# MLP of a two-layer decoder trunk: half of the up product's contraction as seven block products, and the residual summed in DRAM by accumulating transfers

## The chip, the cores and the metric

The kernel runs on one core of a Trainium2 chip. The metric is the time of one execution on the device, in microseconds; three executions are shown and their median is taken.

## The reference

A sequence of 1024 tokens, 1024 channels, everything in float32. Layer 0 mixes with a chunked mLSTM, layer 1 with differential attention over keys and values that are projected once after layer 0. Cut to what the change touches:

```python
def sq_relu_mlp(y, w_up, w_down):                 # w_up 1024x4096, w_down 4096x1024
    return jnp.square(jax.nn.relu(y @ w_up)) @ w_down

for layer in range(2):
    x = x + g1 * mix                              # mLSTM (layer 0), attention (layer 1)
    y = modulate(rms_norm(x, norm_mlp_g[layer]), sh2, sc2)
    x = x + g2 * sq_relu_mlp(y, mlp_w_up[layer], mlp_w_down[layer])
    if layer == 0:
        k1, k2, v = shared_kv(x, ...)             # k and v projections of the normed x
return rms_norm(x, final_norm_g)
```

## The kernel before

**Products.** A float32 value is kept as a rounded high part and the rest, both in the float32r type: `yh` and `yl` for activations, `wh` and `wl` for weights. A product of a 128x128 weight block and 512 tokens is three matmuls into one PSUM bank (`mm3`, lines 183 to 185): `wh` by high, `wh` by low, `wl` by high. The tokens are two halves of 512, the channels eight blocks of 128.

**MLP.** `mlp` goes through the 4096 hidden columns in eight groups of four 128-column tiles. Up phase of a group: four tiles by two halves by eight contraction blocks by three, 192 matmuls. The results go through relu and square (lines 613 and 614). In groups 1 to 7 the hidden values of a pair of tiles are a 2x2 matrix of blocks (tile by token half); `quad_out` forms the sums of blocks that a seven-product scheme for 2x2 matrices needs, and splits them into `bh`, `bl`, `th`, `tl`. `pair_load` does the same to a pair of weight tiles of `w_dn`: raw tiles `e` and `m`, four subtractions and additions of 256 columns (lines 654 to 657), and the splits `eh`, `el`, `lh`, `ll`. Down phase: four pairs `i` by seven products `p` by two contraction blocks by three, 168 matmuls in the order of `PSEQ`. Each product is added to the residual `xt`, which stays in SBUF, by one VectorE instruction on 512 columns (line 675), 28 in a group. Group 8 (the "last" one) uses plain `hh`, `hl`, and its down product goes through `gemm` once for each token half, loading and splitting its weights each time.

**Memory.** Weights pass through a ring of nine tiles of 128x1024 (`wp`); a tile of the ring also serves the modulation's background work (`adar`, line 150). Scratch tiles of 128x512 come from a ring of six (`np_`). PSUM has seven banks for products and one for norms. All loads and stores are issued on SP's queue; POOL has no work.

**Order.** The kernel is written in the order of its data; a scheduler then fixes one order of instructions for each engine, and an instruction waits on semaphores for its inputs and for its output's buffer. Nothing is reordered while it runs.

**Elsewhere.** After layer 0, `gemm` projects queries and then keys, tile order `QKORD`, first group of three tiles; `v_store` writes values to DRAM; `project_a` interleaves the output projection with attention.

Of the kernel before, what the change touches and what calls it, by code (L numbers as in the profile page):

```python
# [17 lines left out]
P = 128  # L18
# [8 lines left out]
FN = 4  # L27
# [3 lines left out]
        (1, 3), (2, 6), (1, 4), (2, 2), (3, 1), (2, 7), (3, 5), (2, 3), (3, 6), (2, 4), (3, 2), (3, 7), (3, 3), (3, 4))  # L31
AHEAD, LAG, FULL, FILL0 = 2, 2, 5, 3
CUT = 256
LSZ = (2, 2, 1, 3)
QKORD = (2, 3, 4, 0, 1, 5, 6, 7)
# [19 lines left out]
def tile_yoco(ctx: ExitStack, tc: tile.TileContext, x, c, pos, cst, vec, bg, lp, ada,  # L55
# [117 lines left out]
    def wload(src, shape, nbg=1, pool=None):  # L173
        r = wp.tile(shape, F32, tag="w", name="wraw")
        sp.dma_start(out=r, in_=src)
        h = (pool or wp).tile(shape, F32R, tag="w", name="wh")
# [29 lines left out]
    def gemm(srcs, nk, ah, al, consume, nbg=1, halves=(0, 1), first=2, hooks=None,  # L206
             after=None, joint=None, sizes=None):
# [5 lines left out]
        def load(g):  # L213
            return [wload(srcs[i], [P, nk, P], nbg) for i in g]
# [382 lines left out]
    def mlp(np_, l, xt, slot, nbg, ends, args, before=None, tail=None, closing=()):  # L597
# [3 lines left out]
        with ExitStack() as ph:  # L601
# [17 lines left out]

            quads = {}  # L620

            def quad_out(f, half, ps):
                j, q = f // 2, quads.setdefault(f // 2, {})
                q[f % 2, half] = squared(ps)
# [13 lines left out]
                if (1, 1) in q:  # L638
# [27 lines left out]

            moving = {1: (bh, bl, 0), 2: (bh, bl, 1), 3: (bh, bl, 2), 4: (th, tl, 3), 5: (th, tl, 0), 6: (th, tl, 1),
                      7: (th, tl, 2)}

            def down(pairs, ready):  # L670
                banks = {}

                def add(ps, half, nb):
                    xs = xt[:, int(half), nb]
                    dve.scalar_tensor_tensor(xs, ps, mcol(l, 5, nb), xs, ALU.mult, ALU.add)  # L675

                for i, p in PSEQ:
# [15 lines left out]
                    add(ps, p in (6, 7, 5, 3), 2 * i + (p in (7, 4, 5)))  # L693
# [27 lines left out]
            for gi in range(FG - 1):  # L721
                srcs = [[dn_src(gi, 2 * i + j, "(p q r c) -> p q r c", q=2, r=2) for j in range(2)] for i in range(4)]
                for got in group_up(gi, w0, steady if gi else first, lambda: pair_load(srcs[0])):
                    if isinstance(got, dict):
                        pairs = [got] + [lambda i=i: pair_load(srcs[i]) for i in range(1, 4)]
                    else:
                        quad_out(*got)
                nxt = []
                down(pairs, lambda: nxt.append(wload(w_up[l, FN * (gi + 1)], [P, NB, P], nbg and nbg + 1)))
                w0 = nxt[0]  # L730
# [3 lines left out]
            sums = hp.tile([P, 2, HT], F32, tag="bh", name="sums")  # L734
            acc[:] = [sums[:, 0], sums[:, 1]]
            srcs = [dn_src(FG - 1, nb, "(p k c) -> p k c", k=FN) for nb in range(NB)]
            gi = FG - 1
            for got in group_up(gi, w0, steady, lambda: None):
                if got is None:
                    continue  # L740
                f, half, ps = got
                r = scratch("r")
# [13 lines left out]
    def resident(ph, name):  # L756
# [5 lines left out]
        return xp.tile([P, 2, NB, HT], F32, tag="x", name="x"), np_  # L762
# [3 lines left out]
    xt, np_ = resident(l0, "1")  # L766
# [15 lines left out]
    def q_norm(half):  # L782
        def f():
            rb = rstd_of(np_, half)
            sp.dma_start(out=rdr[half:half + 1], in_=rb[0:1])
            modulate(np_, xt, rb, half, 3, lambda k: mcol(1, 0, k))
            sp.dma_start(out=xdr[:, half], in_=xt[:, half])
        return f

    mlp(np_, 0, xt, 1, 2, ((0,), (1,)), {(1,): dict(hooks={1: q_norm(0)})}, lambda: scale_cols(3, 48 + 8, V_NMIX + 8),  # L790
# [4 lines left out]

    rps = ExitStack()
    scr = rps.enter_context(tc.tile_pool(name="scr", bufs=2, side="right"))
    cos = scr.tile([P, T], F32, tag="cos", name="cos", bufs=1)
# [39 lines left out]
    def v_store(cc, scr):  # L838
        def f(tb, ps):
            v = scr.tile([P, 2, BV], F32, tag="sv", name="sv")  # L840
            act.copy(out=v, in_=ps.rearrange("p (h v) -> p h v", h=2))  # L841
            for j in range(2):
                sp.dma_start(out=vdr[2 * cc + j, :, tb], in_=v[:, j])
        return f

    q_out = rope_out(lambda s: qdr[:, s], float(BD ** -0.5))
# [6 lines left out]
    def kv_norm(half):  # L853
        return lambda: modulate(np_, xt, kvn[half], half, 2, lambda k: mod[:, 96 + k:97 + k])

    gemm([w_q[n] for n in QKORD], NB, yhk, ylk, q_out, first=3, joint=1,
         after={(3, 0): kv_norm(0), (3, 1): kv_norm(1)})
    gemm([w_kv[n] for n in QKORD], NB, yhk, ylk, rope_out(lambda s: kdr[s], 1.0), first=3, joint=1)
# [22 lines left out]
    with ExitStack() as ph:  # L881
# [6 lines left out]
        identr = ap_.tile([P, P], F32R, tag="identr", name="identr", bufs=1)  # L888
        negr = ap_.tile([P, P], F32R, tag="negr", name="negr", bufs=1)
        neg = ap_.tile([P, P], F32, tag="neg", name="neg", bufs=1)  # L890
        sp.dma_start(out=neg, in_=cst[:, C_NEG])
        act.copy(out=identr, in_=ident)
        act.copy(out=negr, in_=neg)
# [67 lines left out]
        def values(h, qb):  # L961
# [11 lines left out]
            sq = ap_.tile([P, BV], F32, tag="sq", name="sq")  # L973
# [245 lines left out]
```

## Time and profile before

| what | value |
|---|---|
| median of three runs | 2427.49 us (2426.15 to 2429.11) |
| the profiled execution | 2429.98 us, its span 2428.2 us |
| mean granted TensorE clock | 0.991 |
| TensorE busy | 2367.1 us, 12018 matmuls and transposes |
| VectorE busy | 1559.4 us, 2576 instructions |
| ScalarE busy | 989.2 us, 1898 instructions |
| POOL busy | 0.2 us, 4 instructions |
| DMA | 266.81 MB, 110 GB/s on average, all on SP's queue |

The page gives busy time and share of the span by engine, the chain of work that ended last, and groups of instructions with their count, busy time, mean duration in ns, the idle time ahead of them and what ended it. Mean durations include latency that overlaps the next instruction; the pace of an engine is seen from start to start. "PEclk" or the number behind the last engine's busy time is the granted share of TensorE's clock.

### The profile page before, as it was taken

The page shows a single profiled execution, that of the slowest core. Times are in us where ns is not written, and L with a number is a line of the kernel's source. Part 1 is how long each engine was busy: PE and PEld are TensorE (multiplying, and loading weights), DVE is VectorE, ACT ScalarE, POOL GpSimd, SP SyncE. Part 2 cuts the span into 40 slices and gives each one's busy share as a digit, 9 for nine tenths or more (in the row PEclk, how much of TensorE's full clock was granted, in tenths as well). Part 3 has the DMA queues.
Part 4 walks back from the last instruction along what each step waited for, and adds up shares of the span by engine and source line. Part 5 has one row for each costly group of instructions (what it writes and reads, how often), then busy time and mean ns, then how long its engine had stood idle before and what let it go on. Part 6 is the DMA issues. An engine that isn't in the chain of part 4 may idle for free.

```text
span 2428.2 us, 30918 instructions
## 1 busy us (share of the span) xinstructions
PE 2367.1 (97%) x12018; PEld 1983.7 (82%) x12018; DVE 1559.4 (64%) x2576; ACT 989.2 (41%) x1898; POOL 0.2 (0%) x4
## 2 busy tenths in 40 slices
PE   7999999999999999999999999999999999999997
PEld 4899998788888888887788899987778888878886
DVE  7436544787877787767653367664775567566647
ACT  4325633444324323424332467763434323432423
POOL 0000000000000000000000000000000000000000
PEclk9999999999999999999999999999999999999999
DMA  7312242313322342234454654764111111111113
GB/s 306 120 64 77 79 148 78 122 51 119 135 95 79 130 139 75 90 113 143 153 178 154 176 162 148 217 196 160 65 57 35 61 61 44 39 61 57 35 53 122
DMA packets 117150, 266.81 MB, mean 110 GB/s; under 512 B 12426, under 2 KB 51850, under 8 KB 115212
## 3 DMA queue, kind: packets, MB, share of 16 engines
q1 hardware_dynamic: 117004, 264.84, 33.5%
q8 instruction: 94, 1.54, 0.3%
q14 instruction: 52, 0.43, 0.1%
HBM read 228.03 MB, written 36.77 MB: 109 GB/s over the span
## 4 chain that ended last, share of the span: by engine, by line
PE 90%; DVE 3%; DMA 3%; ACT 2%; issue 1%; SPq 1%; DVEq 0%; ACTq 0%
PE gps L183 24%; PE gps L185 24%; PE gps L184 24%; PE gps L255 3%; PE gps L256 3%; PE gps L257 3%; PE gps L971 2%; PE sc L930 1%; PE sc L931 1%; PE tps L957 1%; DMA kb<-kdr 1%; DVE adar L336 1%; PE hps L528 1%; DMA wraw<-in_w_do_dram 1%; PE hps L530 1%
## 5 line engine op out<-in xcount | busy, mean ns | idle before, releaser
L183 PE MATMUL gps<-yh,wh 128*128 128x512 f32 x1664 | 657.4, 399 | 7.9 <-ACT yh L301 5.0
L184 PE MATMUL gps<-yl,wh 128*128 128x512 f32 x1664 | 658.5, 396 | 0.7 <-DVE yl L302 0.7
L185 PE MATMUL gps<-yh,wl 128*128 128x512 f32 x1664 | 655.3, 396 | 0.7 <-DVE wl L171 0.7
L183 PEld LDWEIGHTS gps<-yh,wh 128*128 128x128 f32 x1664 | 313.6, 189 | 85.4 <-ACT yh L301 5.9
L185 PEld LDWEIGHTS gps<-yh,wl 128*128 128x128 f32 x1664 | 313.4, 188 | 78.7 <-DVE wl L171 1.1
L184 PEld LDWEIGHTS gps<-yl,wh 128*128 128x128 f32 x1664 | 313.5, 188 | 76.7 <-issue 1.2
L170 ACT CAST wh<-wraw 128x1024 fp32r<-128x1024 f32 (+2 forms) x176 | 170.6, 970 | 473.7 <-DMA wraw<-in_w_up_dram 208.9
L171 DVE TENSOR_TENSOR wl<-wraw,wh 128x1024 fp32r<-128x1024 f32 (+2 forms) x176 | 198.1, 1126 | 206.3 <-ACT wh L170 204.5
L675 DVE SCALAR_TENSOR_TENSOR x<-gps,mod,x 128x512 f32<-128x512 f32 x392 | 286.8, 746 | 59.7 <-PE gps L185 58.1
L255 PE MATMUL gps<-wh,yh 128*128 128x256 f32 (+1 forms) x768 | 224.9, 293 | 4.8 <-ACT sv L841 3.4
L256 PE MATMUL gps<-wl,yh 128*128 128x256 f32 (+1 forms) x768 | 220.6, 287 | 0.0
L257 PE MATMUL gps<-wh,yl 128*128 128x256 f32 (+1 forms) x768 | 219.9, 286 | 0.0
L170 ACT CAST eh<-e 128x1024 fp32r<-128x1024 f32 x56 | 58.8, 1049 | 240.9 <-DVE e L656 240.9
L150 DVE CUSTOM_DVE_ANT_0 adar<-adar,sil 128x1024 f32<-128x1024 f32 x96 | 117.0, 1223 | 59.8 <-DMA adar<-in_ada_dram 59.2
L255 PEld LDWEIGHTS gps<-wh,yh 128*128 128x128 f32 x768 | 146.7, 191 | 6.5 <-ACT sv L841 3.6
L256 PEld LDWEIGHTS gps<-wl,yh 128*128 128x128 f32 x768 | 146.9, 191 | 1.0
L257 PEld LDWEIGHTS gps<-wh,yl 128*128 128x128 f32 x768 | 146.6, 191 | 0.7
L613 ACT ACTIVATE b<-gps 128x512 f32<-128x512 f32 x112 | 66.9, 597 | 186.9 <-PE gps L185 181.9
L940 ACT ACTIVATE pf<-sc,mx 128x256 f32<-128x256 f32 (+7 forms) x128 | 95.1, 748 | 18.1 <-DVE mx L934 10.4
L171 DVE TENSOR_TENSOR el<-e,eh 128x1024 fp32r<-128x1024 f32 x56 | 68.4, 1222 | 46.2 <-PE gps L184 44.2
L183 PE MATMUL gps<-th,lh 128*128 128x512 f32 x224 | 88.5, 395 | 0.3 <-DVE x L675 0.3
L185 PE MATMUL gps<-th,ll 128*128 128x512 f32 x224 | 88.4, 395 | 0.0
(257 smaller groups left out, 3832.6 us busy)
## 6 DMA issues: line engine op xcount, KB each, us to landing
adar<-in_ada_dram SPq DMA_DIRECT2D x112, 512.0 KB, 4.3
wraw<-in_w_up_dram SPq DMA_DIRECT2D x64, 512.0 KB, 3.3
e<-in_w_dn_dram SPq DMA_DIRECT2D x56, 256.0 KB, 3.0
m<-in_w_dn_dram SPq DMA_DIRECT2D x56, 256.0 KB, 3.0
x<-in_x_dram SPq DMA_DIRECT2D x8, 1024.0 KB, 9.2
wraw<-in_w_mo_dram SPq DMA_DIRECT2D x16, 512.0 KB, 3.2
wraw<-in_w_dn_dram SPq DMA_DIRECT2D x32, 256.0 KB, 2.6
ka<-kdr SPq DMA_DIRECT2D x32, 256.0 KB, 6.8
```

The lines of the kernel that those rows point to most:

```text
L150: dve.tensor_tensor_reduce(r, r, sil, 1.0, 0.0, ALU.mult, ALU.add, mod[:, n:n + 1])
L170: act.copy(out=ph, in_=src)
L171: dve.tensor_tensor(out=pl, in0=src, in1=f32(ph), op=ALU.subtract)
L183: pe.matmul(ps, lhsT=wh, rhs=a, start=first, stop=False, skip_group_check=more)
L184: pe.matmul(ps, lhsT=wh, rhs=b, start=False, stop=False, skip_group_check=more)
L185: pe.matmul(ps, lhsT=wl, rhs=a, start=False, stop=last, skip_group_check=more)
L255: pe.matmul(ps, lhsT=a, rhs=wh[:, k % 4], start=k == 0, stop=False)
L256: pe.matmul(ps, lhsT=a, rhs=wl[:, k % 4], start=False, stop=False)
L257: pe.matmul(ps, lhsT=b, rhs=wh[:, k % 4], start=False, stop=k == NB - 1)
L613: act.activation(dst, ps, AF.Relu)
L675: dve.scalar_tensor_tensor(xs, ps, mcol(l, 5, nb), xs, ALU.mult, ALU.add)
L940: act.activation(pf[f][:, 0:n * P], pp[f][:, 0:n * P], AF.Exp, bias=mx[:, f:f + 1], accum_out=ls[:, f, qb % 4:qb % 4 + 1])
```

## The change

In groups 2 to 7 of each layer, the up products of a pair of tiles are computed in two halves of the contraction. Blocks 0 to 3 form, with the pair's two tiles and the two token halves, two 2x2 block products; each is computed as seven products instead of eight. Blocks 4 to 7 stay plain. That makes 7 x 2 x 3 + 16 x 3 = 90 matmuls for a pair. The weights of a pair come from `up_load`: `pair_load` for the block half, and `praw`, `ph`, `pl` for the plain half. The sums of activation blocks that the scheme needs, `u`, are made once a layer in the down phase of group 1 by `combine` (24 adds, 8 splits, handed out two steps to a product), and take the buffer of `xt`. `up_pair` sums the products in three PSUM banks and, through ScalarE copies and VectorE adds, in scratch tiles (`c11`, `c22`, `c12`).

As `u` takes the buffer of `xt`, the residual moves to DRAM (`xdr`): `xt` is written there at the start of the MLP; in a down phase the first product of each cell goes, multiplied by its gate, into a scratch tile `xs` by ScalarE, the others are added by VectorE, and a finished cell (128x512, 256 KB) is added to `xdr` by an accumulating transfer on POOL's queue, 16 in a group. Before the last group `xt` is read back in four transfers of 1 MB.

Further: the last group's down weights are loaded and split once (`kept`) and serve both token halves; queries and keys are projected with a first group of four tiles (`QSZ`) and a ring of their own for high parts (`wq`); `v_store` writes two token blocks in one transfer; `project_a` has its raw weights fetched ahead; the two constants of the attention mask are made earlier; groups 2 to 7 run their down products in the order `PSEQ2`. All in all 11583 TensorE instructions become 11439.

```diff
-QKORD = (2, 3, 4, 0, 1, 5, 6, 7)
+QKORD = (2, 3, 4, 5, 0, 1, 6, 7)
+QSZ = (4, 2, 2)
...
+            for half in range(l, 2):
+                sp.dma_start(out=xdr[:, half], in_=xt[:, half])
+            u = xp.tile([P, 2, 4, 2, HT], F32R, tag="x", name="u")
...
+            def up_load(f, nbg):
+                pw = pair_load([w_up[l, f + j][:, 0:4].rearrange("p (q r) c -> p q r c", r=2) for j in range(2)])
+                r = wp.tile([P, 2, 4, P], F32, tag="w", name="praw")
+                for j in range(2):
+                    sp.dma_start(out=r[:, j], in_=w_up[l, f + j][:, 4:8])
...
+                split(ph, pl, r)
+                bgwork(nbg)
...
+            def up_pair(pw):
...
+                product(x_, 1, True)
+                c11 = scratch("c11")
+                act.copy(out=c11, in_=x_)
+                product(y_, 5, True)
+                c22 = scratch("c22")
+                act.copy(out=c22, in_=y_)
+                z_ = gps()
+                product(z_, 2, True)
+                product(x_, 6, False)
+                c12 = scratch("c12")
+                act.copy(out=c12, in_=x_)
+                plain(z_, 0, 0, False)
+                plus(c11, z_)
+                yield 0, 0, None, c11
+                product(x_, 7, False)
+                plus(c22, x_)
+                w_ = gps()
+                plain(w_, 1, 1, True)
+                plus(c22, w_)
+                yield 1, 1, None, c22
+                product(y_, 3, False, False)
+                plain(y_, 0, 1, False)
+                plus(c12, y_)
+                yield 0, 1, None, c12
+                plain(x_, 1, 0, False, False)
+                product(x_, 4, False)
+                yield 1, 0, x_, None
...
+                for q in range(2):
+                    b11, b21, b12, b22 = [hl(h, 2 * q + o) for h in range(2) for o in range(2)]
+                    g = diff("t1", b12, b11)
...
+                    put(3, q, v)
...
-                def add(ps, half, nb):
-                    xs = xt[:, int(half), nb]
-                    dve.scalar_tensor_tensor(xs, ps, mcol(l, 5, nb), xs, ALU.mult, ALU.add)
-
-                for i, p in PSEQ:
+                def add(ps, half, nb, again, done):
+                    if not again:
+                        cells[half, nb] = scratch("xs")
+                        act.mul(out=cells[half, nb], in_=ps, mul=mcol(l, 5, nb))
+                    else:
+                        dve.scalar_tensor_tensor(cells[half, nb], ps, mcol(l, 5, nb), cells[half, nb], ALU.mult, ALU.add)
+                    if done:
+                        nc.gpsimd.dma_start(out=xdr[:, half, nb], in_=cells.pop((half, nb)), accum_op=ALU.add)
+
+                for i, p in seq:
+                    for _ in range(2):
+                        next(bg, None)
...
+                if gi:
+                    w1 = up_load(FN * gi + 2, 5 * nbg // 2)
+                    for j, c, ps, cell in up_pair(w0):
+                        quad_out(j, c, ps, cell)
+                    pairs = [pair_load(srcs[0])] + later
+                    for j, c, ps, cell in up_pair(w1):
+                        quad_out(2 + j, c, ps, cell)
...
+                if gi + 1 < FG - 1:
+                    ready = lambda: nxt.append(up_load(FN * (gi + 1), 5 * nbg // 2))
...
+                bg = combine() if gi == 0 else iter(())
+                down(pairs, ready, PSEQ2 if gi else PSEQ, bg)
...
+            xt = xp.tile([P, 2, NB, HT], F32, tag="x", name="x")
+            for half in range(2):
+                for k in range(0, NB, 4):
+                    nc.gpsimd.dma_start(out=xt[:, half, k:k + 4], in_=xdr[:, half, k:k + 4])
...
+            def kept(nb):
+                r = wp.tile([P, 2, FN, P], F32, tag="w", name="raw2")
+                for j in range(2):
+                    sp.dma_start(out=r[:, j], in_=dn_src(gi, nb + j, "(p k c) -> p k c", k=FN))
...
+                split(h2, l2, r)
...
         def project_a():
-            nxt = wload(w_do[0], [P, NB, P], 0)
+            raws = ahead + [wfetch(w_do[1], [P, NB, P])]
+            nxt = wload(None, [P, NB, P], 0, r=raws[0])
...
+                if nb + 2 < NB:
+                    raws.append(wfetch(w_do[nb + 2], [P, NB, P]))
```

VectorE in the down phase of group 1 of layer 0, before: residual updates (line 675), weight preparation (lines 654 to 657 and the splits of line 171), and the tail of the hidden values' splits.

```order
489 L171 TENSOR_TENSOR ll<-m,lh 128x768
490 L675 SCALAR_TENSOR_TENSOR x<-gps,mod,x 128x512
491 L171 TENSOR_TENSOR tl<-v,th 128x512
492 L675 SCALAR_TENSOR_TENSOR x<-gps,mod,x 128x512 x5
493 L654 TENSOR_TENSOR m<-e,m 128x2x128
494 L655 TENSOR_TENSOR e<-m 128x2x128
495 L675 SCALAR_TENSOR_TENSOR x<-gps,mod,x 128x512 x2
496 L656 TENSOR_TENSOR e<-e 128x2x128
497 L675 SCALAR_TENSOR_TENSOR x<-gps,mod,x 128x512
498 L657 TENSOR_TENSOR m<-e 128x2x128
499 L171 TENSOR_TENSOR el<-e,eh 128x1024
```

The same place after the change (line 754 is an add of `combine`, line 173 on `u` its low part, line 808 a residual update of a cell that has had its first result, lines 669 to 672 the weights):

```order
492 L173 TENSOR_TENSOR ll<-m,lh 128x768
493 L808 SCALAR_TENSOR_TENSOR xs<-gps,mod,xs 128x512
494 L173 TENSOR_TENSOR u<-t_4629,u 128x512
495 L754 TENSOR_TENSOR t_4682<-t_4682,yl 128x512
496 L808 SCALAR_TENSOR_TENSOR xs<-gps,mod,xs 128x512
497 L669 TENSOR_TENSOR m<-e,m 128x2x128
498 L670 TENSOR_TENSOR e<-m 128x2x128
499 L754 TENSOR_TENSOR v<-yh 128x512
500 L754 TENSOR_TENSOR t_4629<-yh,t_4629 128x512
501 L808 SCALAR_TENSOR_TENSOR xs<-gps,mod,xs 128x512
502 L754 TENSOR_TENSOR t_4682<-t_4682,yl 128x512
503 L671 TENSOR_TENSOR e<-e 128x2x128
```

Between the four steps of a weight's preparation now stand adds of `combine` and low parts of `u`, and fewer residual updates.

ScalarE in the down phase of a later group of layer 0, before: the casts of the hidden values and of the weights follow each other.

```order
420 L170 CAST th<-t_5713 128x512
421 L170 CAST th<-b 128x512
422 L170 CAST th<-v 128x512
423 L170 CAST eh<-e 128x1024
424 L170 CAST lh<-m 128x768
425 L170 CAST eh<-e 128x1024
426 L170 CAST lh<-m 128x768
427 L170 CAST wh<-wraw 128x1024 x2
```

And after, with the first results of cells (line 806) between them:

```order
636 L172 CAST eh<-e 128x1024
637 L172 CAST th<-t_7879 128x512
638 L172 CAST lh<-m 128x768
639 L806 ACTIVATE xs<-gps,mod 128x512 x4
640 L172 CAST eh<-e 128x1024
641 L172 CAST lh<-m 128x768
642 L806 ACTIVATE xs<-gps,mod 128x512 x3
643 L172 CAST eh<-e 128x1024
644 L172 CAST lh<-m 128x768
645 L806 ACTIVATE xs<-gps,mod 128x512 x3
```

A cast of the next pair's weights now stands behind first results, each of which needs a free scratch tile.

POOL, which had no work of the program's before, after the change (with the semaphores that each transfer waits for; `DMASW` are those of its own earlier transfers):

```order
8 L810 DMA xdr<-xs 128x512 [waits DVE_49] x3
9 L810 DMA xdr<-xs 128x512 [waits Activation_49]
10 L810 DMA xdr<-xs 128x512 [waits DVE_49] x2
11 L810 DMA xdr<-xs 128x512 [waits DMASW0_49,Activation_49]
12 L810 DMA xdr<-xs 128x512 [waits DMASW1_49,DVE_49]
```

From the ninth on, a transfer also waits for the one eight before it.

More of the change, by code (lines that the diff above doesn't have):

```diff
@@ new lines, in umove, with product, plain, plus @@
+            def umove(p, k):
+                if p > 3:
+                    i = (None, None, None, None, 3, 0, 1, 2)[p]
+                    return u[:, 0, i, k], u[:, 1, i, k]
+                half, o = ((0, 0), (0, 1), (1, 1))[p - 1]
+                return yh[:, half, 2 * k + o], yl[:, half, 2 * k + o]
+            def up_pair(pw):
+                x_, y_, z_ = gps(), gps(), None
+                ph, pl = pw["p"]
+                def product(ps, p, first, last=True):
+                    wh, wl, wi = pw[p]
+                    for k in range(2):
+                        a, b = umove(p, k)
+                        mm3(ps, wh[:, k, wi], wl[:, k, wi], a, b, first and k == 0, last and k == 1, not first)
+                def plain(ps, j, half, first, last=True):
+                    for k in range(4):
+                        mm3(ps, ph[:, j, k], pl[:, j, k], yhk(half, 4 + k), ylk(half, 4 + k), first and k == 0,
+                            last and k == 3, not first)
+                def plus(cell, ps):
+                    dve.tensor_tensor(out=cell, in0=ps, in1=cell, op=ALU.add)
+                product(x_, 1, True)
[25 more added lines that the diff above has]
+                yield 1, 0, x_, None
@@ new lines, in combine, with hl, plus, diff @@
+            def combine():
+                def hl(half, k):
+                    return f32(yh[:, half, k]), f32(yl[:, half, k])
+                def plus(out, a, b, op):
+                    dve.tensor_tensor(out=out, in0=a, in1=b, op=op)
+                def diff(name, a, b):
+                    t = scratch(name)
+                    plus(t, a[0], b[0], ALU.subtract)
+                    yield t
+                    plus(t, t, a[1], ALU.add)
+                    yield
+                    plus(t, t, b[1], ALU.subtract)
+                    yield
+                def put(i, q, t):
+                    split(u[:, 0, i, q], u[:, 1, i, q], t)
+                for q in range(2):
+                    b11, b21, b12, b22 = [hl(h, 2 * q + o) for h in range(2) for o in range(2)]
+                    g = diff("t1", b12, b11)
+                    t1 = next(g)
+                    yield
+                    yield from g
+                    put(0, q, t1)
+                    yield
+                    plus(t1, b22[0], t1, ALU.subtract)
+                    yield
+                    plus(t1, t1, b22[1], ALU.add)
+                    yield
+                    put(1, q, t1)
+                    yield
+                    g = diff("t3", b22, b12)
+                    t3 = next(g)
+                    yield
+                    yield from g
+                    put(2, q, t3)
+                    yield
+                    g = diff("v", b21, b11)
+                    v = next(g)
+                    yield
+                    yield from g
+                    plus(v, v, t3, ALU.subtract)
+                    yield
+                    put(3, q, v)
+                    yield
@@ L853, in kv_norm @@
     def kv_norm(half):
[L854 to L858, printed above, removed]
+        return lambda: modulate(np_, res_x[0], kvn[half], half, 2, lambda k: mod[:, 96 + k:97 + k])
+    gemm([w_q[n] for n in QKORD], NB, yhk, ylk, q_out, joint=1, sizes=QSZ, pool=wq,
+         after={(2, 0): kv_norm(0), (2, 1): kv_norm(1)})
+    gemm([w_kv[n] for n in QKORD], NB, yhk, ylk, rope_out(lambda s: kdr[s], 1.0), joint=1, sizes=QSZ, pool=wq)
     token_major(w_vb[0], 256, v_store(0, scr))
@@ L1043, in goal @@
             return due[-1][1]
-        norms, back, begun = [], ([], []), []
+        norms, back, begun, ahead = [], ([], []), [], []
         fill, proj, done = chunks(), project_a(), FILL0
@@ L1057, in tile_yoco @@
                 done += 1
+                if done == ready[1] - 3:
+                    ahead.append(wfetch(w_do[0], [P, NB, P]))
                 if done == ready[1]:
```

118 lines of the change are left out of this document (77 added, 41 removed).

## The prediction

> **What bounds the kernel now.** I read the page's busy table and chain first, then stretches of the two MLPs, then the groups of instructions, and last the places where TensorE stands still.
>
> ```profile
> PE 2367.1 (97%) x12018; PEld 1983.7 (82%) x12018; DVE 1559.4 (64%) x2576; ACT 989.2 (41%) x1898; POOL 0.2 (0%) x4
> PE 90%; DVE 3%; DMA 3%; ACT 2%; issue 1%; SPq 1%; DVEq 0%; ACTq 0%
> ```
>
> TensorE is busy for 97% of the span and is 90% of the chain that ended last. So a matmul removed is time removed wherever TensorE has no wait of its own. That holds in both MLPs, each of which is seven "down" groups and a last one (columns: stretch, length, busy time and count of each engine, granted clock, DMA share, GB/s):
>
> ```profile
> 580.00:1118.00 538.00, 538.00 (x2317) 435.06 (x2317) 395.21 (x616) 185.71 (x269) 0.00 (x0) 1.00 0.31 101
> 1760.00:2330.00 570.00, 569.68 (x2449) 459.26 (x2448) 369.38 (x555) 200.74 (x286) 0.00 (x0) 1.00 0.16 52
> 507.00:546.00 39.00, 39.00 (x169) 31.58 (x168) 37.06 (x58) 13.17 (x19) 0.00 (x0) 1.00 0.18 58
> 1798.70:1837.70 39.00, 39.00 (x168) 31.32 (x168) 23.62 (x34) 12.53 (x16) 0.00 (x0) 1.00 0.23 78
> ```
>
> The first two rows are groups 2 to 8 of each layer: TensorE never stops, at full clock, one 128x512 matmul every 538.00/2317 = 0.232 us (its 396 ns in the groups table is latency that overlaps). VectorE uses 73% and 65%, ScalarE 35%, the DMA engines 31% and 16%: there is room. The last two rows are the down phase of group 1 of layer 0 and of layer 1. In layer 0 VectorE already works 37.06 of 39.00 us there, which matters below. Durations of the work that moves, by group and by start-to-start in the order of time:
>
> ```profile
> L170 ACT CAST wh<-wraw 128x1024 fp32r<-128x1024 f32 (+2 forms) x176 | 170.6, 970 | 473.7 <-DMA wraw<-in_w_up_dram 208.9
> L675 DVE SCALAR_TENSOR_TENSOR x<-gps,mod,x 128x512 f32<-128x512 f32 x392 | 286.8, 746 | 59.7 <-PE gps L185 58.1
> L150 DVE CUSTOM_DVE_ANT_0 adar<-adar,sil 128x1024 f32<-128x1024 f32 x96 | 117.0, 1223 | 59.8 <-DMA adar<-in_ada_dram 59.2
> L613 ACT ACTIVATE b<-gps 128x512 f32<-128x512 f32 x112 | 66.9, 597 | 186.9 <-PE gps L185 181.9
> 503.44 0.68 DVE L171 TENSOR_TENSOR tl<-t,th 128x512 fp32r<-128x512 f32 x1
> 504.04 0.68 DVE L618 TENSOR_TENSOR v<-v,b 128x512 f32<-128x512 f32 x1
> ...
> 506.78 1.22 DVE L171 TENSOR_TENSOR el<-e,eh 128x1024 fp32r<-128x1024 f32 x1
> 507.92 0.68 DVE L171 TENSOR_TENSOR tl<-v,th 128x512 fp32r<-128x512 f32 x1
> 508.52 0.95 DVE L171 TENSOR_TENSOR ll<-m,lh 128x768 fp32r<-128x768 f32 x1
> 509.39 0.68 DVE L618 TENSOR_TENSOR t<-b 128x512 f32<-128x512 f32 x1
> ...
> 522.60 3.37 DVE L675 SCALAR_TENSOR_TENSOR x<-gps,mod,x 128x512 f32<-128x512 f32 x5
> 525.89 0.41 DVE L654 TENSOR_TENSOR m<-e,m 128x256 f32<-128x256 f32 x1
> 526.23 0.41 DVE L655 TENSOR_TENSOR e<-m 128x256 f32<-128x256 f32 x1
> ```
>
> Back to back on VectorE, a 128x512 subtract takes 0.60 us (503.44 to 504.04), 1024 columns 1.14, 768 columns 0.87, 256 columns 0.34, and a residual update (525.89 - 522.60)/5 = 0.66.
>
> **1. Matmuls removed.** A pair of column tiles takes 96 matmuls of the plain form and 90 of the new one. Two pairs, six groups, two layers: 24 x 6 = 144, at 0.232 us: **-33.4 us**. All of it counts if nothing new makes TensorE wait.
>
> **2. Combining yh and yl (group 1).** 24 adds and 8 low parts on VectorE, 32 x 0.60 = 19.2 us; 8 casts go to ScalarE, which has 26 of 39 us idle there. In the same phase 16 of the 28 residual updates leave VectorE, -16 x 0.66 = -10.6. The next group's first load becomes four 256-column adds and splits of 1024, 768 and 1024 columns (4 x 0.34 + 1.14 + 0.87 + 1.14 = 4.5) instead of one of 1024 (1.14): +3.4. Net +12.0 us. Layer 0 has 1.9 us of room, layer 1 15.4. The last part of `u` is wanted by the second product of group 2, so in layer 0 up to 10 us comes out as a wait on TensorE, less what a backlog may slide (the low part of the second weights is wanted later). Ends: 0 and 24 (12 in each layer, no room used). I take 8 in layer 0, near the 10 of its own row, and 2 in layer 1, whose row has room: **+10 us**.
>
> **3. Up products, per group.** ScalarE gets six copies from PSUM (three a pair), VectorE eight adds (4.8 us). With 73% and 35% used these lie beside matmuls. What may be late is a weight: the pair needs nine 128x1024 tiles of a ring of nine, where two plain tiles needed six. By the order of instructions the raw tile of the second pair's plain half gets its buffer 25 matmuls, 5.8 us, ahead of its use; a load and a cast take 3.3 + 0.97 = 4.3:
>
> ```profile
> wraw<-in_w_up_dram SPq DMA_DIRECT2D x64, 512.0 KB, 3.3
> e<-in_w_dn_dram SPq DMA_DIRECT2D x56, 256.0 KB, 3.0
> x<-xdr SPq DMA_DIRECT2D x4, 1024.0 KB, 11.3
> xs<-xdr SPq DMA_DIRECT2D x8, 256.0 KB, 2.9
> xdr<-xs SPq DMA_DIRECT2D x8, 256.0 KB, 2.0
> ```
>
> So it is just in time. Ends 0 and 12 x 3.0 = 36 us (one load of `e` late in every changed group); I take half a microsecond a group, **+6 us**, nearer to zero since 1.5 us is left by the rows.
>
> **4. Residual in DRAM.** Per down phase 16 first results go to ScalarE (16 x 0.60 = 9.6 us, it has 26 idle), and 16 accumulating transfers of 256 KB go out on POOL's queue, which is empty today. They move at most 8.4 MB of reads and writes a group of some 81 us, about as much as the 101 GB/s there now. The wait that this adds: the first-result instruction on ScalarE waits for one of six scratch tiles, and a tile is free only once the transfer of its last user has landed. Behind it on ScalarE stand the casts of the next weights, and TensorE waits for those. No row shows an accumulating transfer. The nearest are the plain write of the same 256 KB, 2.0 us, and the read and the write after each other, 2.9 + 2.0 = 4.9; the far end is x<-xdr, 11.3 us for 1 MB. A pair of column tiles has 4 cells in 42 matmuls, 9.76 us; on average two of the six tiles are being summed in, and four are left for transfers in flight, so the ring sets the pace only if a transfer takes more than 9.76 us. At 4.9, which I take since an accumulation must read and write, it costs **0**. Ends: 0, and at 11.3 us (11.3 - 9.76) x 4 x 14 = +86. The reload of 4 MB a layer is issued a group ahead (45 us of up products cover 11.3); the 2 MB writes at the start of a layer sit on SP between weight loads and are inside the 6 of step 3.
>
> The Trainium skill ("DMA: Bandwidth & Descriptors", section "Anatomy of one DMA — SWDGE (gpsimd) path") fits a transfer issued from GpSimd as about 2.0 us plus bytes over 436 GB/s; that is an estimate of 2.6 us for 256 KB, and the sum would be the same. No run here has yet shown such a transfer.
>
> **5. Stops of TensorE elsewhere.** The other edits (last down weights split once, wider first query group, half as many value stores, the output projection's weights fetched ahead) touch these:
>
> ```profile
> 1122.64 7.37 DMA wraw<-in_w_dn_dram
> 1118.00:1175.00 57.00, 50.39 (x197) 38.28 (x196) 44.71 (x66) 27.55 (x43) 0.00 (x0) 0.94 0.60 200
> 1163.41 0.40 PE L185 MATMUL gps<-yh,wl 128*128 128x512 f32 x1
> 1168.20 2.08 PE L183 MATMUL gps<-yh,wh 128*128 128x512 f32 x4 [4.39 <-ACT yh L301]
> ...
> 1173.91 0.45 PE L184 MATMUL gps<-yl,wh 128*128 128x512 f32 x1
> 1340.00:1420.00 80.00, 74.29 (x563) 70.99 (x563) 39.88 (x81) 43.18 (x133) 0.00 (x0) 0.96 0.57 154
> 1505.00:1610.00 105.00, 99.95 (x745) 93.73 (x744) 73.40 (x156) 72.54 (x239) 0.00 (x0) 0.98 0.79 226
> 1610.00:1690.00 80.00, 73.86 (x391) 62.28 (x392) 45.66 (x72) 40.86 (x92) 0.00 (x0) 0.94 0.40 143
> ```
>
> TensorE is idle 6.6, 5.7, 5.1 and 6.1 us in the four stretches. After the stop that ends at 1168.20, 13 matmuls take 5.71 us up to 1173.91 where 3.02 would do: a stop costs 2.7 us more, and the granted clock of that stretch is 0.94. The Trainium skill ("TensorE: Matmul & The Clock Gate", "What's actually happening") has the clock halve after an idle window of about 3.4 us; the trace agrees, with 0.43 us between matmuls after 4.39 us of idle. By that rule, a wait of step 2 that comes in one piece costs 2.7 us on top, and one in crumbs does not. A query group of four gives 24 more matmuls, 5.6 us, to cover the norm that TensorE waits for, more than 4.39: -5 of the 4.39 + 2.7. The value stores and the prefetch take parts of the other stretches: -2 and -3. Ends 0 and -20 (most of 23.5 idle); I take **-10 us**.
>
> **The sum.** -33.4 + 10 + 6 + 0 - 10 = -27.4. The profiled execution took 2429.98 us, 2.5 above the median of the runs, 2427.49; so 2429.98 - 27.4 - 2.5 = **2400 us**.
>
> **Rivals.** A. *Accumulations set the pace (slower).* One mechanism: six scratch tiles in the down phases, refilled only as transfers land. Each microsecond beyond 9.76 costs 4 x 14 = 56 us, so the gain of 27.4 is gone at 10.2 us, and at 10.6 us the time is 2400 + 47 = 2447. The same holds if POOL's queue can start one only every 2.44 us or slower. For it: an accumulation reads, adds and writes, and 11.3 us for 1 MB shows that this chip's DRAM traffic can be slow. Against it: 2.0 and 2.9 for the same size. The Trainium skill ("SBUF — State Buffer", "SBUF: two separate sides") warns that some VectorE copies keep GpSimd from writing its descriptors, which would act just so; no run here shows it. Chance 0.14.
>
> B. *The new preparation costs half of the gain.* Step 2 at its upper end (24) plus two half-rate pieces (5.4), step 3 at 6, gaps as taken: 2400 + 19.4 = 2419, some way to no change. For it: VectorE's 37.06 of 39.00. Against: layer 1's 15.4 us of room. Chance 0.22, of which 0.05 within the bound of no change.
>
> C. *Everything new is hidden and the stops go.* -33.4 - 20: 2430 - 53.4 - 2.5 = 2374. For it: the full rows of groups 2 to 8. Against: step 2 in layer 0. Chance 0.10.
>
> **How the numbers follow.** The forecast has 0.52, A 0.14, B 0.22, C 0.10, and 0.02 is left for no gain at all. Three runs spread over 3 us, so 0.2%, 4.9 us, is about what can be told from no change. Faster: 0.52 + 0.10 + 0.17 = 0.79; the same 0.07; slower 0.14. The range takes in B, half of C and the nearest part of A, 2374 to 2430, and leaves out 0.05 + 0.12 + 0.02 of chance; the likeliest case by itself spans 2390 to 2411.
>
> **What would show it.** Step 1: 144 fewer 128x512 matmuls at the same pitch in groups 2 to 7 (a group of 80.8 us instead of 83.6). Step 2: VectorE full in the down phase of layer 0's group 1, and matmuls that read `u` or the new weights waiting for it; none in layer 1. Step 4: landing times of xdr<-xs at 3 to 6 us; were they 9 or more, ScalarE's first results would wait for DMA and rival A holds. Step 5: no stop of 4 us ahead of the query product. The prediction is wrong if waits in groups 2 to 7 exceed 6 us in sum, or if the accumulating traffic slows the weight loads (3.0 and 3.3 us now).

## The result, and the profile after

The change makes the kernel slower: 2545.62 us (median of four runs, 2537.81 to 2549.04) against 2428.3 us beside it, a ratio of 1.0475 (95% interval 1.0453 to 1.0497). That is 117 us more where 27 less were forecast. Of the page after, the busy table, the DMA queues (packets, MB, share of 16 engines' time; q0 is POOL's) and the chain:

```profile
PE 2382.6 (94%) x11874; PEld 1971.0 (77%) x11874; DVE 1551.9 (61%) x2608; ACT 1172.1 (46%) x2210; POOL 198.7 (8%) x236
q1 hardware_dynamic: 123580, 266.94, 32.4%
q0 software_dynamic: 33408, 67.12, 16.9%
PE 67%; DMA 15%; DVE 10%; ACT 4%; issue 3%; SPq 0%; POOL 0%; DVEq 0%; ACTq 0%; POOLq 0%
```

There are 144 fewer matmuls (12018 to 11874), as forecast, yet TensorE is busy 15.5 us longer and idle 163.8 us instead of 61.1. Its share of the chain falls from 90% to 67%, and 15% of the chain is now DMA. The stretches that hold five groups of layer 0 and of layer 1, from the start of one down phase to the sixth, before and after:

```profile
595.50:1013.70 418.20, 418.20 (x1802) 338.04 (x1801) 318.03 (x500) 146.87 (x210) 0.00 (x0) 1.00 0.33 107
1862.30:2281.20 418.90, 418.83 (x1802) 337.77 (x1801) 267.67 (x401) 147.95 (x210) 0.00 (x0) 1.00 0.16 51
```
```profile
607.40:1099.10 491.70, 434.84 (x1742) 337.64 (x1741) 317.30 (x520) 214.79 (x332) 68.87 (x80) 0.95 0.60 139
1956.00:2397.20 441.20, 416.58 (x1741) 329.59 (x1740) 264.33 (x412) 218.54 (x331) 69.55 (x80) 0.98 0.48 96
```

A group took 83.6 us in layer 0 and 83.8 in layer 1; it takes 98.3 and 88.2, where 80.8 was to be. VectorE does no more than before (317 us against 318), ScalarE has room, the granted clock is 0.95 and 0.98, and the DMA share has gone from 0.33 to 0.60 and from 0.16 to 0.48, at a mean rate of 139 GB/s instead of 107 and 96 instead of 51. Whom TensorE waits for in the whole span (engine and line, releaser, us in total, times, longest):

```profile
PE gps L190 <- ACT eh L172: 34.7, 19, 4.0
PE gps L190 <- ACT xs L806: 32.7, 27, 2.3
PE gps L190 <- DVE c L718: 22.6, 8, 4.9
```

Casts of weights, first results, and the adds that sum up-products: work that was hidden before. One place in layer 0 shows how it hangs together (five rows of its timeline):

```profile
829.97 0.54 SPq L668 DMA_DIRECT2D m<-in_w_dn_dram  x1
...
835.70 0.43 DVE L669 TENSOR_TENSOR m<-e,m 128x256 f32<-128x256 f32 x1 [4.71 <-DMA m<-in_w_dn_dram]
...
837.00 1.05 ACT L172 CAST eh<-e 128x1024 fp32r<-128x1024 f32 x1 [3.76 <-DVE e L671]
837.30 0.74 DVE L808 SCALAR_TENSOR_TENSOR xs<-gps,mod,xs 128x512 f32<-128x512 f32 x1
...
838.10 0.50 PE L190 MATMUL gps<-bh,eh 128*128 128x512 f32 x1 [0.46 <-ACT eh L172]
```

The load lands 5.7 us after its issue. VectorE, whose order is fixed, stands 4.71 us in front of it; behind it wait the weight's cast on ScalarE and a residual update that frees a PSUM bank, and in the end TensorE waits for the cast, here for 0.46 us. The landing times in groups 2 to 7 of layer 0, after and before:

```profile
xdr<-xs POOLq DMA_DIRECT2D x81, 256.0 KB, 5.3
e<-in_w_dn_dram SPq DMA_DIRECT2D x22, 256.0 KB, 5.4
```
```profile
e<-in_w_dn_dram SPq DMA_DIRECT2D x23, 256.0 KB, 3.1
```

In layer 1 the same loads hardly move (3.2 us instead of 3.0 in the median). There the loads of `e` for the up products are late: 4.4 us, where they take 2.7 in the run with plain writes below.

### The profile page after: what moved, and what is told of

Same layout as the page of the kernel before. It is cut to its first block, busy times and chain, and to the rows that moved or that the text cites. A ratio compares the mean times of both kernels' runs of the same rounds, so it can differ in the third digit from the quotient of the medians.

```text
span 2546.4 us, 31886 instructions
## 1 busy us (share of the span) xinstructions
PE 2382.6 (94%) x11874; PEld 1971.0 (77%) x11874; DVE 1551.9 (61%) x2608; ACT 1172.1 (46%) x2210; POOL 198.7 (8%) x236
## 3 DMA queue, kind: packets, MB, share of 16 engines
q0 software_dynamic: 33408, 67.12, 16.9%
## 4 chain that ended last, share of the span: by engine, by line
PE 67%; DMA 15%; DVE 10%; ACT 4%; issue 3%; SPq 0%; POOL 0%; DVEq 0%; ACTq 0%; POOLq 0%
PE gps L190 17%; PE gps L191 17%; PE gps L192 16%; DMA adar<-in_ada_dram 4%; DMA m<-in_w_dn_dram 4%; PE gps L262 3%; PE gps L263 3%; PE gps L264 3%; PE gps L1154 2%; DMA praw<-in_w_up_dram 1%; PE sc L1113 1%; PE sc L1114 1%; PE tps L1140 1%; DMA kb<-kdr 1%; DMA m<-in_w_up_dram 1%
## 5 line engine op out<-in xcount | busy, mean ns | idle before, releaser
L810 POOL DMA_DIRECT2D xdr<-xs x224 | 194.0, 892 | 2209.4 <-DVE xs L808 2085.7
L190 PE MATMUL gps<-yh,wh 128*128 128x512 f32 x896 | 350.9, 399 | 7.6 <-ACT wh L172 4.1
L192 PE MATMUL gps<-yh,wl 128*128 128x512 f32 x896 | 354.5, 397 | 2.5 <-DVE wl L173 2.5
L191 PE MATMUL gps<-yl,wh 128*128 128x512 f32 x896 | 355.9, 398 | 0.8 <-DVE yl L309 0.8
L806 ACT ACTIVATE xs<-gps,mod 128x512 f32<-128x512 f32 x224 | 147.4, 686 | 272.7 <-PE gps L192 232.3
L190 PEld LDWEIGHTS gps<-yh,wh 128*128 128x128 f32 x896 | 169.0, 189 | 51.0 <-ACT wh L172 5.2
L191 PEld LDWEIGHTS gps<-yl,wh 128*128 128x128 f32 x896 | 168.9, 189 | 41.9 <-issue 1.2
L190 PE MATMUL gps<-yh,ph 128*128 128x512 f32 x384 | 158.9, 414 | 28.7 <-DVE c L718 22.6
L191 PE MATMUL gps<-yl,ph 128*128 128x512 f32 x384 | 156.3, 407 | 0.0
L192 PE MATMUL gps<-yh,pl 128*128 128x512 f32 x384 | 151.7, 408 | 0.3
L172 ACT CAST eh<-e 128x1024 fp32r<-128x1024 f32 x80 | 83.6, 1044 | 108.6 <-DVE e L671 106.4
```

What stands on the lines that cost most here:

```text
L172: act.copy(out=ph, in_=src)
L190: pe.matmul(ps, lhsT=wh, rhs=a, start=first, stop=False, skip_group_check=more)
L191: pe.matmul(ps, lhsT=wh, rhs=b, start=False, stop=False, skip_group_check=more)
L192: pe.matmul(ps, lhsT=wl, rhs=a, start=False, stop=last, skip_group_check=more)
L806: act.mul(out=cells[half, nb], in_=ps, mul=mcol(l, 5, nb))
L810: nc.gpsimd.dma_start(out=xdr[:, half, nb], in_=cells.pop((half, nb)), accum_op=ALU.add)
```

## The experiments

Four theories were set up. T1: the adding transfers hold the DMA engines and slow the weight loads beside them. T2: the fixed order of instructions and the ring of nine tiles cost, whatever the transfers do. T3, a part of T2: five background tiles in a row. T4, later H: first results on ScalarE.

**No transfers.**

```diff
-                        nc.gpsimd.dma_start(out=xdr[:, half, nb], in_=cells.pop((half, nb)), accum_op=ALU.add)
+                        cells.pop((half, nb))
```

> The changed kernel without its 224 accumulating transfers: a finished cell is dropped, so the down products do not reach the residual; every other step stands. The scheduler orders anew. Theory T1 (the transfers take DMA engines from the weight loads, which land late): the time falls by most of the excess of 117 + 33 us, to 2395 to 2430 us, and loads of e and m in groups 2 to 7 land in about 3 us again. Rival T2 (the fixed order of ScalarE and VectorE and the nine-tile ring that one pair of up weights fills are to blame): the time stays above 2490 us, with ScalarE's first results and casts still ahead of TensorE's stops.

2480.3 us, ratio 1.0218 (1.0192 to 1.0245): 65 us of the excess go, and 94 stay above the 2386 that the kernel with only the small parts (below, 2419.4) less 33.4 for the matmuls would give. In layer 0's groups the loads of `e` and `m` of the down weights land in 3.1 and 3.2 us, where the changed kernel has 5.4 and 4.3. The time lies between the two expected ranges, so neither theory is enough alone.

**Plain writes for adding ones.** The order of all engines is the same, row by row.

```diff
-in_=cells.pop((half, nb)), accum_op=ALU.add)
+in_=cells.pop((half, nb)))
```

> The 224 transfers stay, on the same queue, but write plainly instead of adding, so xdr holds the last cell instead of the sum; the order of every engine is the same, row by row. T1 in its strong form (an accumulation reads and writes DRAM and holds the DMA engines longer than a write of the same bytes): landing falls from 5.2 to about 2.5 us, loads land earlier, and a good half of the excess goes, to 2420 to 2480 us. T2, or if the queue on POOL itself is what costs: within 20 us of 2546.

2489.0 us, 1.0255 (1.0234 to 1.0276), 9 us above the range of T1 and far below that of T2. So in this kernel the adding alone costs 57 us. The same bytes written plainly cost some 9 more than none, which is little beside the spread of the runs, and without transfers the engines' orders are others. The queue and the landing time, to be held beside 16.9% and 5.2 us:

```profile
q0 software_dynamic: 19072, 67.12, 7.2%
xdr<-xs POOLq DMA_DIRECT2D x224, 256.0 KB, 2.6
```

TensorE's waits for casts of `eh`, 34.7 us with adding transfers, are nearly gone, while those for the adds `c` (23.1 us) and for first results (27.3) stay:

```profile
PE gps L190 <- ACT eh L172: 4.1, 6, 1.6
```

The 8.39 MB of the reload, the queue's only work in the run without transfers, are 0.8% of the engines' time; the other 58.7 MB then take some 16.1% when they add and 6.4% when they write, 2.5 times as much, and land in 5.2 us instead of 2.6. This answers the fit of the Trainium skill that the prediction gave ("DMA: Bandwidth & Descriptors", "Anatomy of one DMA — SWDGE (gpsimd) path", an estimate of 2.6 us): the estimate holds for the plain write and misses the adding one by a factor of two.

**Plain up products, residual in DRAM.** `up_load` and `up_pair` give way to the old up phase, `combine` goes.

```diff
-                    w1 = up_load(FN * gi + 2, 5 * nbg // 2)
-                    for j, c, ps, cell in up_pair(w0):
...
+                for got in group_up(gi, w0, steady if gi else first, lambda: pair_load(srcs[0])):
```

> Residual in DRAM by accumulating transfers as in the changed kernel, but the up products of all groups plain (192 matmuls a group, wload for each tile, no u, no combine). Against the kernel before it has 0 matmuls fewer. T1: the transfers cost by themselves, so this is slower than before by 40 to 100 us (2470 to 2530). T2 (the up products' nine-tile loads and their order cost): within 15 us of before, 2410 to 2440.

2498.4 us, 1.0293 (1.0272 to 1.0313), in the range of T1. The residual in DRAM costs by itself.

**Only the small parts.** As the last one, with the residual back in SBUF:

```diff
-                        nc.gpsimd.dma_start(out=xdr[:, half, nb], in_=cells.pop((half, nb)), accum_op=ALU.add)
...
+                    xs = xt[:, half, nb]
+                    dve.scalar_tensor_tensor(xs, ps, mcol(l, 5, nb), xs, ALU.mult, ALU.add)
```

> Only the other parts of the change: last down weights split once, query and key groups of four, two value blocks a store, output weights fetched ahead, constants made early; residual in SBUF and up products plain as before. The prediction's step 5 took 10 us off for these (ends 0 and 20): 2410 to 2425 us. If they cost in the changed kernel, slower than 2428.

2419.4 us against 2428.7, 0.9967 (0.9954 to 0.9981): 9.3 us faster, the best version here. So the residual in DRAM costs 79 us (2498.4 - 2419.4). TensorE's waits no longer have the query norm's 4.4 us. And the block products on top of both cost 47 us (2545.6 - 2498.4) instead of saving.

**Plain up products and plain writes.** The edit of the plain write, on the kernel with plain up products and the residual in DRAM.

> Plain up products and residual in DRAM (the kernel that took 2498 us, 79 above the one with only the small parts, 2419), but each finished cell is written plainly instead of added, so xdr holds the last cell and not the sum. Theory T1 (the adding itself is what costs: 2.5 times the engine time of a plain write, loads that land late): most of the 79 us goes, 2430 to 2450. Rival T4 (ScalarE's first results stand behind casts and hold the PSUM bank that TensorE adds into next): at least half stays, 2458 to 2485.

2431.7 us, 1.0012 (1.0001 to 1.0022), in the range of T1: 67 of the 79 us are the adding, 12 are left for the transfers as such and the first results on ScalarE. Against this kernel the one with plain writes and block products (2489.0) is 57 us slower, although it has 144 matmuls fewer.

**Adding traffic that nothing depends on.** The small parts' kernel, and each finished residual cell is also added to a tensor that is never read (it is filled once, ahead of layer 0's groups):

```diff
...
+                    if done:
+                        nc.gpsimd.dma_start(out=xdr2[:, half, nb], in_=xs, accum_op=ALU.add)
```

> The kernel with only the small parts (2419 us; residual in SBUF, plain up products, right results), plus the same 16 adding transfers of 256 KB a down phase on POOL's queue, each taking a finished cell of the residual to a DRAM tensor that nothing reads, so no scratch tile and no result hangs on them. Theory T1a (the adding transfers slow the weight loads beside them): 2450 to 2490, with weight loads landing later and TensorE waiting for casts of weights. Rival T1b (only the scratch tiles that come free late cost): within 10 us of 2419.

2476.1 us, 1.0211 (1.0174 to 1.0249): 57 us more, with no scratch tile involved, where T1b had at most 10. The 57 us hold the bytes as well as the adding, and the scheduler made another order; plain writes were not tried on this kernel. Landing times in layer 0's groups, without and with the traffic, and who waits there with it:

```profile
wraw<-in_w_up_dram SPq DMA_DIRECT2D x24, 512.0 KB, 4.4
e<-in_w_dn_dram SPq DMA_DIRECT2D x24, 256.0 KB, 3.1
```
```profile
wraw<-in_w_up_dram SPq DMA_DIRECT2D x22, 512.0 KB, 6.2
e<-in_w_dn_dram SPq DMA_DIRECT2D x24, 256.0 KB, 4.0
```
```profile
DVE m L669 <- DMA m<-in_w_dn_dram: 44.3, 18, 4.7
PE gps L191 <- DVE x L805: 17.4, 12, 2.4
```

Loads are late, VectorE stands in front of them for 44 us (25 without the traffic), and TensorE waits for the residual updates behind. The expectation had named casts of weights in their place.

**Background work spread** (on the plain-write kernel, layer 0 only).

```diff
-up_load(FN * (gi + 1), 5 * nbg // 2)
+up_load(FN * (gi + 1), nbg)
...
+                    got = pair_load(srcs[i])
+                    bgwork(nbg if gi else 0)
```

> The changed kernel with plain writes (2489 us; xdr holds the last cell and not the sum), with the background work of layer 0's groups 2 to 7 in pieces of two behind each weight load instead of five behind each pair of up weights; the scheduler orders anew. Theory T3 (five background tiles in a row pass through the nine-tile ring behind a load that fills it, and VectorE stands waiting for them ahead of the adds that free PSUM banks; layer 0's groups take 91 us and layer 1's 87): layer 0's groups fall to layer 1's, 2460 to 2470. Rival (the up weights themselves are late): within 8 us of 2489.

2474.7 us, 1.0185 (1.0156 to 1.0214): 14 us, where T3 said 19 to 29. The five groups of layer 0 fall from 463.1 us to 442.4 and those of layer 1, which have no background work, from 430.8 to 427.5. The profiled execution took 6 us less than the median, so these differences are somewhat large. TensorE's waits for the adds `c` in layer 0 (22.5 us) are gone, but 11.9 us for residual updates and 7.5 for casts of `eh` (1.6 before) have come in their place. Layer 0 does not come down to layer 1, so T3 is a part only.

**First results on VectorE**, all of them (on the plain-write kernel), then that with spread background work and adding transfers, then only two of sixteen (on the plain-write kernel with spread background work).

```diff
-                        act.mul(out=cells[half, nb], in_=ps, mul=mcol(l, 5, nb))
+                        dve.tensor_scalar(out=cells[half, nb], in0=ps, scalar1=mcol(l, 5, nb), scalar2=None, op0=ALU.mult)
```

> The changed kernel with plain writes (2489 us; xdr holds the last cell and not the sum), with the first result of each cell made by VectorE instead of ScalarE; the scheduler orders anew. T4: the stops that end with ScalarE's first result (about 10 us in groups 2 to 7 of each layer and what they cost after in half-rate matmuls) go, 2445 to 2475. Rival: VectorE, 62 of some 93 us in layer 0, gets 16 more instructions a group and becomes late itself: 2485 to 2510.

> The changed kernel, adding transfers as they are, with both: first results on VectorE and the background work spread. If T3 and T4 add up beside the transfers' price of 57 us: about 2546 - 25 - 25 = 2496, between 2475 and 2515. If the slow transfers hide the two (the loads are late anyway): 2525 to 2550.

> The kernel with plain writes and spread background work (2475 us; xdr holds the last cell and not the sum), with only the first two first results of each down phase (the first pair's products 1 and 5) on VectorE, the other 14 on ScalarE. Theory H (the handover from the up to the down phase: on ScalarE these two stand behind relu, square and casts of the last hidden block, and TensorE's next product needs their banks; 2.0 us a group plus half-rate matmuls behind it): the stops that end with ScalarE's first result go, 2440 to 2460. Rival (VectorE is as late there, as when it had all first results, 2534): 2475 to 2500.

2534.4 us (1.0436), 2582.4 us (1.0632) and 2494.1 us (1.0256): slower by 45, 37 and 19 us than the kernels they start from, 2489, 2545.6 and 2475. That is slower than any range said for the first two (2510 and 2550 at most); only the third lies in its rival's range. What the rivals said of VectorE, that it becomes late itself, fits each time. In the third, TensorE waits at the same place 3.1 us for VectorE's two where it had waited 2.1 for ScalarE's.

**Another order of down products.**

```diff
-PSEQ2 = ((0, 1), (0, 5), (1, 1), (0, 6), (0, 2), (1, 5), (0, 7), (0, 3), (1, 6)) + PSEQ[9:]
+PSEQ2 = ((0, 1), (0, 5), (1, 1), (1, 5), (0, 6), (0, 2), (0, 7), (0, 3), (1, 6)) + PSEQ[9:]
```

> The kernel with plain writes and spread background work (2475 us; xdr holds the last cell and not the sum), with the down products of groups 2 to 8 in another order: the second pair's product 5 comes ahead of the first pair's product 6, so the first pair's bank is used again one product (1.4 us) later. Theory H: the stop of about 2 us at the handover shrinks by up to 1.4 us in twelve groups and its half-rate tail with it, 2445 to 2465. Rival (the stop waits for a weight or a hidden block, not for the bank; or the second pair's weights now come late): 2470 to 2490.

2477.3 us, 1.0200 (1.0175 to 1.0224), no change and in the rival's range, but no evidence against H, for the order did not change where it matters: the second pair's weights were not there, so the scheduler put the first pair's product 6 back in the same place. The stop in the spread kernel and then here, in the same group:

```profile
2064.65 0.40 PE L192 MATMUL gps<-th,el 128*128 128x512 f32 x1
2067.16 0.50 PE L190 MATMUL gps<-th,eh 128*128 128x512 f32 x1 [2.12 <-ACT xs L806]
2067.50 0.39 PE L191 MATMUL gps<-tl,eh 128*128 128x512 f32 x1
2067.73 0.39 PE L192 MATMUL gps<-th,el 128*128 128x512 f32 x1
```
```profile
2071.55 0.71 PE L190 MATMUL gps<-th,eh 128*128 128x512 f32 x1 [2.12 <-ACT xs L806]
2072.06 0.63 PE L191 MATMUL gps<-tl,eh 128*128 128x512 f32 x1
2072.49 0.63 PE L192 MATMUL gps<-th,el 128*128 128x512 f32 x1
```

**First results first.** On the spread kernel: the first two down products are written ahead of the last hidden block, and that block's relu may only be issued behind their first results.

```diff
...
+                        if cell is None:
+                            next(steps)
+                            next(steps)
+                            with tc.issue_after(firsts[-1].ins):
+                                quad_out(2 + j, c, ps, cell)
```

> The kernel with plain writes and spread background work (2475 us; xdr holds the last cell and not the sum), written so that in groups 2 to 7 the first two down products and their first results come ahead of the last hidden block; on ScalarE the two first results then stand before that block's relu, square and cast, and nothing moves to VectorE. Theory H (ScalarE's fixed order at the handover holds the bank that TensorE needs): the stop of about 2 us a group and its half-rate tail go, 2435 to 2460. Rival (some other input is as late): 2468 to 2485, with the stop ending on another releaser.

2456.4 us, 1.0120 (1.0089 to 1.0152): 18 us, and H holds, at the upper end of its range. What ScalarE did in the spread kernel while TensorE stood from 2065.0 to 2067.2, and layer 1's wait there and here:

```profile
2064.61 0.60 ACT L620 ACTIVATE b<-gps 128x512 f32<-128x512 f32 x1
2065.24 0.63 ACT L621 ACTIVATE b<-b 128x512 f32<-128x512 f32 x1
2065.91 0.62 ACT L172 CAST bh<-b 128x512 fp32r<-128x512 f32 x1
2066.43 1.26 ACT L806 ACTIVATE xs<-gps,mod 128x512 f32<-128x512 f32 x2
```
```profile
PE gps L190 <- ACT xs L806: 12.0, 6, 2.1
```
```profile
PE gps L190 <- ACT xs L808: 4.7, 6, 0.8
```

The matmuls of the first pair's product 1 had ended at about 2058; its result stood in the bank until ScalarE took it at 2066.43. ScalarE had idle time between, but in its fixed order the first result stood behind the last hidden block.

**`combine` without its adds**, also on the spread kernel: `u` is split from plain blocks.

```diff
-                    t = scratch(name)
-                    plus(t, a[0], b[0], ALU.subtract)
-                    yield t
...
+                    yield a[0]
```

> The kernel with plain writes and spread background work (2475 us; xdr holds the last cell and not the sum), with combine's 24 adds a layer left out: u is split from plain blocks, so the up products are of wrong sums; the 8 splits and all matmuls stand. The prediction's step 2 has VectorE's load in the first down phase cost 8 us in layer 0 and 2 in layer 1; the profile shows stops of 4.8 and 4.6 us there and half-rate matmuls of 4.4 and 1.2 us. If VectorE's load is the cause: 2460 to 2467. If it is ScalarE's first results there too: 2470 to 2477.

2467.2 us, 1.0142 (1.0116 to 1.0169), 7.5 us less, at the edge of the range for VectorE's load; with three runs each (2468 to 2477 and 2460 to 2467) this is rough. The first down phase of layer 0 in the spread kernel and here:

```profile
511.50:561.00 49.50, 44.72 (x175) 32.82 (x174) 49.04 (x82) 26.60 (x40) 8.26 (x15) 0.97 0.37 126
```
```profile
511.50:561.00 49.50, 48.33 (x204) 37.59 (x203) 33.11 (x52) 23.96 (x35) 8.22 (x15) 1.00 0.41 138
```

VectorE was full (49.04 of 49.50 us) and TensorE idle for 4.8 us; with the adds left out VectorE works 33.11 us and TensorE is idle for 1.2. In layer 1's first down phase TensorE's waits fall from 4.5 us to 0.8.

## Why the prediction was wrong, step by step

**Step 1, -33.4 us.** Right as far as it goes: 144 matmuls fewer. What failed is its condition, "if nothing new makes TensorE wait", and that idle time makes the matmuls behind it slower. TensorE's busy time rose by 15.5 us where it was to fall by 33.4, so the others took 49 us longer; by an estimate from the granted clock (0.991 over the span before and 0.977 after, so 23 and 58 us lost), some 35 of these come from the clock. The 15.5 us and the 103 us of new idle time make the 118 us by which the span grew. The sign that the prediction named, more than 6 us of waits in groups 2 to 7, came: TensorE is idle for 57 us in the five groups of layer 0 above and for 25 in those of layer 1. Its step 5 let a stop slow the matmuls behind it only when it came in one piece of the length of 4.39 us; the last section has what shorter stops did.

**Step 2, +10 us.** Right as far as tested: 7.5 us in the run without the adds, which is rough, and VectorE full as forecast. The split between the layers was not as forecast: layer 1's row looked roomy and waited too.

**Step 3, +6 us.** Mis-sized: the term that failed second. Block products on top of all else cost 47 us where steps 1 to 3 had 17 off, so if the 33.4 count in full, steps 2 and 3 together are some 81 us and not 16. Step 3 priced one late load and took the room of VectorE and ScalarE over a whole group (73% and 35%) as cover. That room is no cover when an engine in a fixed order stands before one late input. The runs found 14 us for the bunched background work and 18 for the handover on ScalarE, which belongs to step 4's first results and was named there only as queueing behind scratch tiles. The slack of 1.5 us that step 3 had left was reckoned with the 3.3 us of `wraw` over the whole run; in layer 0's groups these loads took 4.4 already in the kernel with only the small parts.

**Step 4, 0 us.** The step that failed first: the residual in DRAM costs 79 us. The landing time was well forecast (4.9 against 5.2 us). The ring of six did not set the pace: ScalarE's first results waited for a landing nine times, 19.0 us in all, but TensorE waited for first results 32.7 us with adding transfers and 27.3 with plain ones, so rival A's mechanism is not what cost the time, though its sign was right. What was priced at nothing is what the transfers do to others. The prediction counted bytes, "about as much as the 101 GB/s there now", and named slower weight loads only as a sign of being wrong; it should have counted engine time, and asked which loads stand beside them with how much slack. The slack left in step 3 was 1.5 us, and in layer 0 loads of `e` came 2.3 us later. The price of the adding is 57 us in the changed kernel and 67 with plain up products, in the same order of matmuls each time. Traffic that nothing depends on cost 57 us by itself, its bytes included.

**Step 5, -10 us.** Right in sum: -9.3 us. The query norm's wait went as forecast. TensorE's wait for the value stores did not shrink (3.4 us before, 3.8 with only the small parts), and a wait of the attention for ScalarE that the prediction had not named fell from 6.5 us to 1.2, so the split was partly luck.

**What adds up and what stays open.** -33.4 (matmuls) - 9.3 (small parts) + 57 (adding) + 12 (plain transfers and first results) + 14 (background) + 18 (handover) + 7.5 (`combine`) = +66 of +117. These come from runs on different bases and need not add exactly. Put on step by step, in one order, the parts do add: -9 (small parts), +79 (residual in DRAM), +47 (block products) make +117. What is not taken apart lies in the block products: about 51 us remain. The best repaired kernel, 2456 us with plain writes, is still 25 us slower than plain up products with plain writes (2431.7). In it a group takes 87.5 us in layer 0 and 84.2 in layer 1 instead of 80.8, in waits of 0.2 to 2 us for residual updates, casts of weights and the splits of the last hidden block. No run took these apart; that they all come from orders fixed ahead is argued, not shown.

## What to carry to other kernels

Price a transfer by the time it takes from the DMA engines and by the slack of the loads beside it, not by its bytes or its own landing time: here the adding transfers took 2.5 times the engine time of plain writes, and such traffic cost 57 us without anything waiting for it. Where each engine's order is fixed, look at handovers between phases for the instruction that frees a bank and what stands ahead of it; free time on average does not help it. And test a saving together with what it displaces: the block products were worth 33 us by count, and their own preparation and what made room for them each cost more.

## What the runs showed of the hardware

An adding transfer of 256 KB landed in 5.2 us in the changed kernel and a plain one from the same queue in 2.6 (medians of 224), and POOL was busy 0.87 us with issuing the one and 0.54 with the other (69.55 and 43.36 us for 80).

A stop of 2.1 us can be enough to halve TensorE's pace. The two fences of the run with another order of down products show the same stop, 2.12 us before the same matmul, once with matmuls 0.23 us apart behind it and once 0.43; the granted clock of the 3.5 us behind it is 1.00 and 0.52. Take all fifteen traces and every stop of 0.5 us or more ahead of five 128x512 matmuls in a row: the mean granted clock of the 3 us behind it was below 0.8 after 101 of 131 stops of 2.0 to 3.5 us, after all 45 longer ones, and after 52 of 413 shorter than 2.0. The changed kernel has 219 matmuls of 128x512 that take more than 0.55 us, the kernel before 83. The Trainium skill ("TensorE: Matmul & The Clock Gate", "What's actually happening") has the clock halve after an idle window of about 3.4 us and calls the window free-running. That length is too long for these traces; a free-running window would fit the stop that has a tail here and none there, but no run shows the window itself.
